# An encoder layer whose instruction order a planner sets: looser bounds on who takes a place, another first wave, and four more places

## The chip, the cores and the metric

The kernel runs on one core of a Trainium2 chip. The core has TensorE (PE in the profile, with its weight loads as PEld), VectorE (DVE), ScalarE (ACT), GpSimd (POOL), and SyncE (SP), which here issues nearly all DMAs. The metric is the device time of one execution in microseconds; the kernel before takes 2035.23 us (median of three runs, 2032.91 to 2036.42).

## The reference

One layer of an encoder on a sequence of 2048 tokens with 1024 features, in float32. The mixer is windowed attention with 16 query heads and 4 key/value heads, a sink logit for each head and a relative-position bias; a SwiGLU with 2816 hidden units follows. Shift, scale and gate of each sub-layer come from a conditioning vector `c` (adaLN):

```python
c_act = jax.nn.silu(c)
mod = (c_act @ ada_w[i] + ada_b[i])[:, None, :]
sh1, sc1, g1, sh2, sc2, g2 = jnp.split(mod, 6, axis=-1)
h = rmsnorm(x, mix_norm_pre[i]) * (1.0 + sc1) + sh1
y = windowed_gqa_sink(h, att_w_qkv[j], att_w_o[j], att_sink[j], rel_bias)
x = x + g1 * rmsnorm(y, mix_norm_post[i])
h = rmsnorm(x, ffn_norm_pre[i]) * (1.0 + sc2) + sh2
x = x + g2 * rmsnorm(swiglu(h, ffn_w_in[i], ffn_w_out[i]), ffn_norm_post[i])
```

`rmsnorm` divides by the root of the mean square over the 1024 features. `mod` is a product of a 1024-vector with a 1024x6144 matrix.

## The kernel before

**Layout.** Features lie on the 128 partitions, so a 512-token chunk of x is eight tiles of 128x512 (`x0_0` to `x0_7` for chunk 0), and there are four chunks. A product in float32 accuracy is made of three fast ones: each operand is split into a high part `hi` (a rounding cast on ACT) and a low part `lo` (the rest, a subtraction on DVE or POOL), and `three` issues w_hi·h_hi, w_hi·h_lo and w_lo·h_hi, each 128x512. A product of two plain float32 operands is also possible; the trace shows it as two records of a matmul.

**Stages.** (1) *The first wave.* Chunk 0 is loaded, squared on ACT, added in pairs on DVE, and three plain float32 matmuls with a matrix of ones sum the squares over the partitions (`squares0`, `rstd_of`). ACT and DVE make the reciprocal root `nr` of it. Then, for each of the eight feature tiles k: two rows of `ada_w` are loaded and reduced against silu(c) on DVE (`ada_reduce`, a custom instruction 1024 wide, which the trace calls CUSTOM_DVE_ANT_0) to give scale (`mod` 8+k, then `coef` k) and shift (`mod` k); 896 columns of the query/key/value weights for k are loaded and split (`w_piece`, tiles `w0_k`; the raw columns and the `ada_w` rows share five places, `raws`); x_k is multiplied by `nr` on DVE, scaled and shifted on ACT, and split; and 21 matmuls (seven output tiles by three) add feature tile k into seven PSUM banks. The remaining 640 columns (`w1_k`) come after. (2) The rest of the projections of chunks 0 and 1. (3) Attention in 64 units of 128 queries and one key/value head. Under its first half PE is filled up with the projections of chunks 2 and 3, under its second half with the output projections of chunks 0 to 2 (class `OProj`, tiles `ol` and `wo`): each unit pulls about 18 or 20 such matmuls (`Budget`, `FILL`). (4) `OProj` of a chunk writes eight tiles y, sums their squares (`yacc`, squares in `nsq` tiles), takes their norm (`nhio`, `nloo` are the two matmuls of that sum), adds x (`residual`), squares and sums again (`xacc`), takes the second norm (`nhix`, `nlox`), and makes the FFN's input h2 (`make_h2`), which goes through HBM. (5) The output projection of chunk 3, without attention beside it. (6) The FFN, with a Strassen-like scheme of seven products in place of eight, from about 700 us to the end.

**What sets the order.** None of the code above issues an instruction. `Recorder` notes every call in program order; `schedule` then runs a list scheduler (`forward`, with a cost in ns for each operation) and a backward pass that gives each operation a due time, eighteen times over, replays each order with random DMA delays, and keeps the best. `emit` writes the instructions in that order (line 748, so nearly every row of the profile has that line), with each on its engine's queue; an engine works its queue strictly in that order. Tiles with the same tag of the same pool share a number of places (`bufs`). In `forward` an operation that is the first to touch a tile can only be placed when the tile can have a place, and the places of a tag are given out strictly in recorded order:

```python
def slot_of(b):
    t = b.tag
    if t.order[t.next] is not b:
        return None
```

The PSUM pool `psF` has one tag, `mm`, with two banks. Under attention's second half its tiles are, in recorded order, the `py` tiles of the output projection (24 matmuls each) and, between them, the `nst` tiles of the norm sums. A `py` tile recorded behind a norm sum cannot take a bank before that norm sum has taken its own, which it does with its first matmul. In the pool `yp` the tag `y` has twelve places and `nsq`, the square tiles, four.

Of the kernel before, what the change touches and what calls it, by code (L numbers as in the profile page):

```python
# [20 lines left out]
P = 128  # L21
S = 2048
D = 1024
# [33 lines left out]

HOLD = 6
# [8 lines left out]
SPARE = 800.0  # L67

# [16 lines left out]
class Buf:  # L85


    def __init__(self, rec, name, shape, dtype, pool, tag):
# [3 lines left out]
        self.log, self.ops, self.slot, self.real = [], set(), None, None  # L92

# [42 lines left out]
class Recorder:  # L136
# [41 lines left out]
    def record(self, eng, fn, args, kw):  # L178
# [13 lines left out]
        if fn == "matmul" and not kw.get("start"):  # L192
            op.reads.append(op.writes[0])
        elif fn == "matmul":
            op.writes = [(op.writes[0][0], (3, (1 << P) - 1))]
# [13 lines left out]
        for w, items in ((False, op.reads), (True, op.writes)):  # L209
            for b, m in items:  # L210
# [3 lines left out]
                if b.tag is not None and op not in b.ops:  # L214
# [3 lines left out]
                    op.tiles.append(b)  # L218
        op.succ = []
# [26 lines left out]
    def cost(self, op, outs, ins):  # L246
# [12 lines left out]
        elif eng == "pe":  # L259
            if fn == "transpose":  # L260
                op.occ, op.lat = 108, 330
            elif outs[0].dtype == F32 and ins[0].dtype == F32:
                op.occ, op.lat = 860 * n // CH, 1060 * n // CH
# [79 lines left out]
    def forward(self, ahead, spare):  # L343


        for t in self.tags:
            t.next, t.held, t.free = 0, [None] * t.bufs, [0.0] * t.bufs
            t.parked = []
# [12 lines left out]
        def slot_of(b):  # L361
            t = b.tag
            if t.order[t.next] is not b:
# [53 lines left out]
        while n < len(ops):  # L417
# [119 lines left out]
            for b in o.tiles:  # L537
                t = b.tag
                b.end = max(b.end, end)
                if b.slot is None:  # L540
# [4 lines left out]
                    t.next += 1  # L545
                    wake(t)
# [209 lines left out]

def row(ap, n):
# [5 lines left out]
def encoder_layer(ctx, tc, a):  # L763
# [36 lines left out]
    gains = constr.tile([P, 4, KT], F32, name="gains")  # L800
    nsink = const.tile([P, HEADS], F32, name="nsink")
# [8 lines left out]
    def rstd_of(alloc, psp, ptag, acc, tag, r=None, direct=False, short=False, keep=False):  # L810
# [5 lines left out]
        if direct or len(sums) > 1:  # L816
            for i, sq in enumerate(sums):
                pe.matmul(ps, f(ones), sq, start=i == 0, stop=i == len(sums) - 1)
        else:
# [10 lines left out]
        if short:  # L830
# [3 lines left out]
            dve.scalar_tensor_tensor(out, t, 1.5, r, ALU.add, ALU.mult)  # L834
            return out
# [26 lines left out]
    class Chunk:  # L862
# [20 lines left out]
        def squares0(self):  # L883
# [6 lines left out]
            dve.tensor_tensor(sq[6], sq[4], sq[6], ALU.add)  # L890
            self.acc = [sq[0], sq[2], sq[6]]

        def norm(self, psp, ptag):
            r = nrm.tile([P, CH], F32, tag="nr", name=f"nr{self.c}")
            self.r = rstd_of(rot(nrm, "nsq", 2), psp, ptag, self.acc, f"a{self.c}", r)
# [41 lines left out]
    with ExitStack() as pa:  # L937
        w2 = open_pool(pa, "w2", side="right")
        raws = open_pool(pa, "raws", 5, side="right")
        w1 = open_pool(pa, "w1", side="right")  # L940
        psA = open_pool(pa, "psA", 8, space=PSUM)

        cb = nrm.tile([P, D], F32, name="cb")
        sp.dma_start(cb, row(a["c"], D))
        ch0 = Chunk(0)
        sp.dma_start(adab, a["ada_b"])
        sp.dma_start(gains, a["gains"])
        act.activation(cb, cb, AF.Silu)
# [9 lines left out]

        wres = {}
# [896 lines left out]
```

## Time and profile before

| | |
|---|---|
| median of three runs | 2035.23 us |
| the profiled execution, its own time | 2033.44 us |
| its span, first to last instruction | 2031.6 us |
| mean granted TensorE clock | 0.997 |
| PE, DVE, ACT, POOL busy in the span | 98%, 83%, 53%, 28% |
| DMA moved | 415.23 MB, mean 204 GB/s |

The page gives the busy share of each engine in 40 slices of some 51 us, the DMA queues, the chain of work that ended last and the costliest groups of instructions. A matmul's end is modelled, so PE counts as busy while matmuls follow one another at whatever spacing; the number of matmuls that start in a stretch, and the distance of their starts, tell more than the share.

### The profile page before, as it was taken

How to read it: one execution, taken by the hardware profiler on the slowest of the kernel's cores; microseconds unless marked ns; L12 is line 12 of the kernel's file. 1: busy time of each engine (PE TensorE's matmuls, PEld its weight loads, DVE VectorE, ACT ScalarE, POOL GpSimd, SP SyncE). 2: the span in 40 equal slices, each digit the busy share in tenths (PEclk: the TensorE clock that was granted, in tenths of full speed). 3: DMA queues.
4: the chain of work that ended last, by engine and by line, in shares of the span. 5: the costliest groups of instructions: out<-in, count | busy, mean ns of one | idle time of the engine just before them, and what ended most of it. 6: DMA issues, size and time to landing. Idle time of an engine off the chain costs nothing.

```text
span 2031.6 us, 29024 instructions
## 1 busy us (share of the span) xinstructions
PE 1995.9 (98%) x9392; PEld 1663.1 (82%) x9392; DVE 1689.8 (83%) x3051; ACT 1072.0 (53%) x2099; POOL 571.7 (28%) x520
## 2 busy tenths in 40 slices
PE   6999999999999999999999999999999999999999
PEld 4888888888787878788888888888888888888888
DVE  7868888877989888988887998776776789989997
ACT  5557766777778864344343533333333744455433
POOL 1302442344657513432333231111111000120034
PEclk9999999999999999999999999999999999999999
DMA  9895765576777694444446743333233794398543
GB/s 312 307 331 198 241 210 173 195 279 227 254 272 257 225 363 152 160 161 165 166 158 244 272 151 134 117 137 106 83 124 101 236 335 152 108 331 300 174 156 110
DMA packets 208581, 415.23 MB, mean 204 GB/s; under 512 B 19964, under 2 KB 61997, under 8 KB 205357
## 3 DMA queue, kind: packets, MB, share of 16 engines
q1 hardware_dynamic: 207852, 412.84, 59.1%
q8 instruction: 75, 1.23, 0.2%
q14 instruction: 78, 0.63, 0.1%
q10 hardware_dynamic: 576, 0.52, 0.1%
HBM read 278.52 MB, written 134.77 MB: 203 GB/s over the span
## 4 chain that ended last, share of the span: by engine, by line
PE 65%; DVE 2%; DMA 1%; issue 1%; ACT 0%; POOL 0%; SPq 0%; ACTq 0%; DVEq 0%; POOLq 0%
PE bank L748 65%; DMA hb<-h_d 0%; DVE pr L748 0%; DMA wor<-w_o 0%; DVE u_i L748 0%; DVE y L748 0%; DVE plo L748 0%; DMA ly<-y_d 0%; DMA lx<-xT 0%; DVE ly L748 0%; POOL ly L748 0%; DVE ws_i L748 0%; DVE wa_i L748 0%; SPq L748 0%; DVE of L748 0%
## 5 line engine op out<-in xcount | busy, mean ns | idle before, releaser
L748 PE MATMUL bank<-ht,ws_i 128*128 128x512 f32 x1584 | 374.0, 389 | 0.0
L748 PEld LDWEIGHTS bank<-ht,ws_i 128*128 128x128 f32 x1584 | 297.3, 188 | 61.7
L748 PE MATMUL bank<-hb,wa_i 128*128 128x512 f32 x1056 | 254.1, 389 | 0.5 <-DVE hb L748 0.5
L748 PEld LDWEIGHTS bank<-hb,wa_i 128*128 128x128 f32 x1056 | 198.1, 188 | 42.0 <-DVE hb L748 0.9
L748 PE MATMUL bank<-ol,wo 128*128 128x512 f32 x768 | 206.1, 396 | 2.1 <-ACT yacc L748 1.1
L748 DVE TENSOR_TENSOR u_i<-bank,u_i 128x512 f32<-128x512 f32 x176 | 120.9, 688 | 80.3 <-PE bank L748 77.7
L748 ACT CAST ws_i<-s_i 128x512 fp32r<-128x512 f32 x132 | 81.9, 621 | 192.9 <-DVE s_i L748 96.8
L748 ACT ACTIVATE pr<-pr,nm 128x385 f32<-128x385 f32 (+1 forms) x256 | 154.8, 606 | 53.2 <-DVE nm L748 48.0
L748 DVE CUSTOM_DVE_ANT_0 pr<-bank,bias,nsink 128x384 f32<-128x384 f32 (+1 forms) x256 | 149.8, 594 | 25.3 <-PE bank L748 21.7
L748 POOL TENSOR_SCALAR pr<-pr,rs 128x384 f32<-128x384 f32 (+1 forms) x177 | 114.6, 660 | 179.7 <-DVE rs L748 167.9
L748 PEld LDWEIGHTS bank<-ol,wo 128*128 128x128 f32 x768 | 141.2, 188 | 28.5 <-ACT yacc L748 1.5
L748 POOL TENSOR_TENSOR p_i<-p_i,u_i 128x512 f32<-128x512 f32 x41 | 66.9, 1633 | 346.3 <-DVE u_i L748 176.0
L748 POOL TENSOR_TENSOR z<-z,z 128x512 f32<-128x512 f32 x28 | 43.8, 1572 | 337.4 <-ACT ws_o L748 263.2
L748 PE MATMUL bank<-k,q 128*128 128x384 f32 (+1 forms) x512 | 135.4, 344 | 1.5 <-DVE nm L748 1.4
L748 PE MATMUL bank<-hi,ws 128*128 128x512 f32 x384 | 134.3, 400 | 0.0
L748 DVE TENSOR_TENSOR plo<-bank,phi 128x512 fp32r<-128x512 f32 x184 | 120.7, 684 | 11.2 <-ACT phi L748 10.1
L748 ACT CAST wa_i<-wiri 128x512 fp32r<-128x512 f32 x132 | 81.3, 620 | 90.8 <-PE bank L748 77.6
L748 PE MATMUL bank<-hb,ws_i 128*128 128x512 f32 x528 | 126.9, 389 | 1.6 <-ACT p_i L748 1.6
L748 PE MATMUL bank<-ht,wa_i 128*128 128x512 f32 x528 | 126.8, 389 | 0.0
L748 DVE TENSOR_TENSOR z<-bank,z 128x512 f32<-128x512 f32 (+1 forms) x164 | 107.7, 659 | 17.9 <-PE bank L748 16.5
L748 DVE TENSOR_TENSOR wa_i<-wiri,wa_i 128x512 fp32r<-128x512 f32 x132 | 103.8, 788 | 19.1 <-ACT wa_i L748 19.1
L748 PEld LDWEIGHTS bank<-hb,ws_i 128*128 128x128 f32 x528 | 99.0, 188 | 22.5 <-ACT p_i L748 2.0
(275 smaller groups left out, 4434.5 us busy)
## 6 DMA issues: line engine op xcount, KB each, us to landing
wiri<-w_in SPq DMA_DIRECT2D x88, 512.0 KB, 4.6
ada<-ada_w SPq DMA_DIRECT2D x40, 512.0 KB, 5.3
q_d<-e SPq DMA_DIRECT2D x32, 512.0 KB, 4.6
q<-q_d SPq DMA_DIRECT2D x16, 1024.0 KB, 7.0
wo<-wo_d SPq DMA_DIRECT2D x16, 1024.0 KB, 6.0
wiro<-w_out SPq DMA_DIRECT2D x40, 384.0 KB, 4.4
g_d_b<-p_i SPq DMA_DIRECT2D x44, 256.0 KB, 3.4
g_d_t<-p_i SPq DMA_DIRECT2D x40, 256.0 KB, 2.0
```

The lines of the kernel that those rows point to most:

```text
L748: o.ins = getattr(engs[o.eng], o.fn)(*args, **kw)
```

## The change

Three things at once.

1. *Places in the order of readiness, within bounds.* For the tags listed in `LOOSE` (`psF`'s `mm` and `yp`'s `nsq`, each 4) a tile may take a place ahead of up to four that were recorded before it, but not ahead of one of its own family (names that begin with the same letters: `py`, `nst`, `psq`). All other tags stay strict.
2. *A new first wave.* The rows of `ada_w` get a pool of their own with sixteen places (`raws0`), and the pool of the `w1_k` tiles is opened when it closes, in the same space. For k = 0 (`ADA_PE = 1`) shift and scale are plain float32 matmuls with one moving column: eight for each, on a copy of `ada_w` laid out for it, and silu(c) as a 128x8 tile `ct`. The low parts of the `w0_k` split are fixed on DVE. The squares are summed in four matmuls in place of two additions and three matmuls. The norm's chain is the short form (one ACT square less). For chunk 0 `hi` is written by ACT straight from the scaled x, with a second activation for x itself, in place of an activation and a cast. And `busy` adds matmuls that nobody reads, into a PSUM tile `warm`: 14 at the start, 6 behind the first sum of squares, 5 and 8 behind two DVE steps of the norm.
3. *Sixteen places* for `y` in place of twelve.

```diff
+ADA_PE = 1
+WARM = {"ones": 14, 0: 6, "t": 5, "r": 8}
+LOOSE = {("psF", "mm"): 4, ("yp", "nsq"): 4}
...
+            t.left = list(t.order)
+            skip = LOOSE.get((t.pool.name, t.name), 0)
+            t.reach = skip + 1
...
             t = b.tag
-            if t.order[t.next] is not b:
+            for x in t.left[:t.reach]:
+                if x is b:
+                    break
+                if x.family == b.family:
+                    return None
+            else:
                 return None
...
+            if fill is not None:
+                fill("t", t)
+                fill("r", r)
             return out
...
-            dve.tensor_tensor(sq[6], sq[4], sq[6], ALU.add)
-            self.acc = [sq[0], sq[2], sq[6]]
+            self.acc = sq[::2]
...
-            act.activation(xt, xt, AF.Identity, bias=mod[:, k:k + 1], scale=coef[:, 0, k:k + 1])
+            if c == 0:
+                act.activation(hi, xt, AF.Identity, bias=mod[:, k:k + 1], scale=coef[:, 0, k:k + 1])
+            act.activation(xt, xt, AF.Identity, bias=mod[:, k:k + 1], scale=coef[:, 0, k:k + 1])
+            if c == 0:
+                return scaled, dve.tensor_tensor(lo, xt, f(hi), ALU.subtract)
...
-        w2 = open_pool(pa, "w2", side="right")
         raws = open_pool(pa, "raws", 5, side="right")
         w1 = open_pool(pa, "w1", side="right")
+        first = ExitStack()
+        raws0 = open_pool(first, "raws0", KT * C2 * 2 // D, side="right")
...
+        def ada_products(k):
+            for e, t in enumerate((8 + k, k)):
+                w = raws0.tile([P, D], F32, tag="raw", name=f"adat{t}")
+                sp.dma_start(w, a["ada_t"][t])
+                j = 2 * k + e
+                for i in range(KT):
+                    pe.matmul(ada_ps[:, j:j + 1], w[:, i * P:(i + 1) * P], ct[:, i:i + 1],
+                              start=i == 0, stop=i == KT - 1)
+                dve.tensor_tensor(mod[:, t:t + 1], ada_ps[:, j:j + 1], adab[:, t:t + 1], ALU.add)
...
-            split(t[:, 0], t[:, 1], w[:, :n], pool)
+            split(t[:, 0], t[:, 1], w[:, :n], pool if i else dve)
...
+        def busy(what, src):
+            for _ in range(WARM.get(what, 0)):
+                pe.matmul(warm[:, :P], f(ones), src[:, :P], start=True, stop=True)
...
-                y = yp.tile([P, CH], F32, tag="y", name=f"y{c}_{n}", bufs=4 if c == NCH - 1 else 12)
+                y = yp.tile([P, CH], F32, tag="y", name=f"y{c}_{n}", bufs=4 if c == NCH - 1 else 16)
```

The planner draws the whole order anew from this, so nearly every queue differs. Three places follow, each as the queue stood and as it stands now.

*PE, the start of the program, before* (`nsq` are the pairs of squares, `hi0_0` is feature tile 0 of chunk 0):

```order
L748 MATMUL bank0<-nsq0_0_86,ones_57 128x512
L748 MATMUL bank0<-nsq0_2_95,ones_57 128x512
L748 MATMUL bank0<-nsq0_6_115,ones_57 128x512
L748 MATMUL bank1<-hi0_0_164,w0_0_137 128x512
L748 MATMUL bank2<-hi0_0_164,w0_0_137 128x512
```

*and in the change* (`adat` are the rows of `ada_w` for k = 0; the matmuls into bank0 up to `hi0_0` are the ones nobody reads):

```order
L767 MATMUL bank0<-ones_57 128x128 x14
L767 MATMUL bank1<-nsq0_0_103,ones_57 128x512
L767 MATMUL bank0<-nsq0_0_103,ones_57 128x128 x6
L767 MATMUL bank1<-nsq0_2_114,ones_57 128x512
L767 MATMUL bank1<-nsq0_4_128,ones_57 128x512
L767 MATMUL bank1<-nsq0_6_138,ones_57 128x512
L767 MATMUL bank2<-mod_64,adat8_105 128x1 x8
L767 MATMUL bank2<-mod_64,adat0_112 128x1 x8
L767 MATMUL bank0<-nta0_175,ones_57 128x128 x5
L767 MATMUL bank0<-nr0_154,ones_57 128x128 x8
L767 MATMUL bank3<-hi0_0_206,w0_0_173 128x512
```

Behind the sums of squares there are now 16 one-column matmuls and 13 unread ones before the first projection.

*DVE in the first wave, before* (`ISA ada` is the reduction of a row of `ada_w`, `ISA mod` reads its sum, `lo` and `w0` are low parts of a split):

```order
L748 TENSOR_TENSOR lo0_0_176<-x0_0_64,hi0_0_164 128x512
L748 TENSOR_TENSOR x0_2_72<-x0_2_72,nr0_129 128x512
L748 TENSOR_TENSOR w0_2_180<-wqkv2_0_150,w0_2_180 128x896
L748 ISA ada11_162,mod_132<-ada11_162,cb_84,adab_88 128x1024
L748 ISA mod_132 128x1
L748 ISA ada2_146,mod_132<-ada2_146,cb_84,adab_88 128x1024
L748 ISA mod_132 128x1
L748 ISA ada10_139,mod_132<-ada10_139,cb_84,adab_88 128x1024
L748 ISA mod_132 128x1
L748 TENSOR_TENSOR lo0_1_220<-x0_1_70,hi0_1_194 128x512
L748 SCALAR_TENSOR_TENSOR coef_152<-mod_132,gains_117 128x1
L748 TENSOR_TENSOR x0_3_74<-x0_3_74,nr0_129 128x512
```

*and in the change:*

```order
L767 TENSOR_TENSOR lo0_0_225<-x0_0_71,hi0_0_206 128x512
L767 SCALAR_TENSOR_TENSOR coef_186<-mod_64,gains_131 128x1
L767 TENSOR_TENSOR x0_1_75<-x0_1_75,nr0_154 128x512
L767 TENSOR_TENSOR w0_1_220<-wqkv1_0_145,w0_1_220 128x896
L767 ISA ada10_149,mod_64<-ada10_149,cb_126,adab_101 128x1024
L767 ISA mod_64 128x1
L767 TENSOR_TENSOR lo0_1_253<-x0_1_75,hi0_1_236 128x512
L767 ISA ada2_158,mod_64<-ada2_158,cb_126,adab_101 128x1024
L767 ISA mod_64 128x1
L767 SCALAR_TENSOR_TENSOR coef_186<-mod_64,gains_131 128x1
L767 TENSOR_TENSOR x0_2_78<-x0_2_78,nr0_154 128x512
L767 TENSOR_TENSOR w0_2_255<-wqkv2_0_167,w0_2_255 128x896
```

Before, some low parts of the weights are missing here (k = 1, 5, 6 and 7 stood in POOL's queue); now DVE's queue goes round with the same six operations, and the two reads of a sum, for k = 1 to 4: reduction, `lo`, reduction, `coef`, x, `w0`.

*PE under attention's second half, around the second norm sum of chunk 0 (`nhix0`, `nlox0`), before* (`ol,wo` is output projection, all other rows but the norm sum are attention):

```order
L748 MATMUL bank7<-plo9_3_2_5721,v2_3_5120 128x512
L748 MATMUL bank4<-ident_59,pr10_3_5513 128x128
L748 MATMUL bank5<-ident_59,pr10_3_5513 128x128
L748 MATMUL bank6<-ident_59,pr10_3_5513 128x128
L748 MATMUL bank3<-k3_0_5308,q3_0_5301 128x384 x2
L748 MATMUL bank2<-k3_0_5308,q3_0_5301 128x384 x2
L748 MATMUL bank1<-nhix0_5747,ones_57 128x512
L748 MATMUL bank0<-ol1_0_4217,wo1_4_5528 128x512 x4
L748 MATMUL bank1<-nlox0_5750,ones_57 128x512
L748 MATMUL bank0<-ol1_0_4217,wo1_4_5528 128x512 x2
```

*and in the change:*

```order
L767 MATMUL bank1<-ol1_2_5099,wo1_5_5645 128x512 x4
L767 MATMUL bank3<-k3_0_5360,q3_0_5356 128x384 x2
L767 MATMUL bank1<-ol1_2_5099,wo1_5_5645 128x512
L767 MATMUL bank5<-ident_59,pr10_3_5541 128x128
L767 MATMUL bank4<-ident_59,pr10_3_5541 128x128
L767 MATMUL bank6<-ident_59,pr10_3_5541 128x128
L767 MATMUL bank1<-ol1_3_5126,wo1_5_5645 128x512 x3
L767 MATMUL bank0<-nhix0_5847,ones_57 128x512
L767 MATMUL bank5<-ident_59,pr10_3_5541 128x128
L767 MATMUL bank1<-ol1_3_5126,wo1_5_5645 128x512 x2
```

Before, no `ol,wo` row stands in the 27 rows ahead of `nhix0`: the next one, `wo1_4`, begins right behind it. Now `wo1_4` and `wo1_5` begin ahead of the norm sum; behind `nlox0` one more `ol,wo` row stands, and then 17 rows of attention alone up to `wo1_6`.

More of the change, by code (lines that the diff above doesn't have):

```diff
@@ L218, in record @@
                     op.tiles.append(b)
+        if eng == "pe" and op.writes[0][0].group is not None:
+            for q in op.writes[0][0].group:
+                op.pred.setdefault(q, 0)
+            op.writes[0][0].group = [op]
         op.succ = []
@@ L970, in w_piece @@
                 wres[k, "v"] = (t[:, 0, :2 * P], t[:, 1, :2 * P])
+        warm = psA.tile([P, CH], F32, tag="mm", name="warm")
+        def busy(what, src):
+            for _ in range(WARM.get(what, 0)):
+                pe.matmul(warm[:, :P], f(ones), src[:, :P], start=True, stop=True)
+        busy("ones", f(ones))
         ch0.squares0()
-        ch0.norm(psA, "mm")
+        ch0.norm(psA, "mm", busy)
         steps = []
```

38 lines of the change are left out of this document (30 added, 8 removed).

## The prediction

> **What bounds the kernel now.** I read the page first, then the chain, then windows by stage, then the timeline where the windows show a loss.
>
> ```profile
> span 2031.6 us, 29024 instructions
> PE 1995.9 (98%) x9392; PEld 1663.1 (82%) x9392; DVE 1689.8 (83%) x3051; ACT 1072.0 (53%) x2099; POOL 571.7 (28%) x520
> 841.41 1177.96 PE bank L748 x5280
> ```
>
> PE is the bound: busy 98%, and from 841 us to 2019 us the chain is one unbroken run of matmuls. The change hardly touches those, so a gain can only come from the 36 us in which PE idles and from matmuls that run at half clock. The windows say where both are:
>
> ```profile
> 0.00:50.00 50.00, 29.70 (x99) 19.80 (x100) 38.33 (x63) 28.02 (x37) 6.83 (x9) 1.00 0.91 312
> 50.00:54.00 4.00, 4.00 (x12) 3.13 (x11) 4.00 (x4) 0.95 (x2) 1.34 (x1) 0.57 0.82 269
> 550.00:560.00 10.00, 7.18 (x29) 4.83 (x28) 8.68 (x22) 7.30 (x17) 7.34 (x7) 0.77 0.79 265
> 560.00:570.00 10.00, 9.80 (x44) 7.79 (x43) 8.28 (x20) 4.86 (x12) 6.50 (x8) 0.89 0.59 206
> 600.00:620.00 20.00, 20.00 (x111) 17.24 (x110) 18.56 (x48) 16.00 (x39) 7.16 (x11) 1.00 0.80 275
> 640.00:660.00 20.00, 18.20 (x96) 14.43 (x96) 19.73 (x52) 18.34 (x45) 15.80 (x17) 1.00 0.87 282
> 690.00:720.00 30.00, 27.47 (x117) 21.27 (x116) 24.77 (x30) 22.56 (x35) 12.83 (x9) 1.00 1.00 364
> 1000.00:1200.00 200.00, 200.00 (x884) 165.62 (x883) 175.29 (x247) 84.58 (x142) 65.47 (x43) 1.00 0.59 208
> ```
>
> The columns are stretch, length, then busy time and count of PE, PEld, DVE, ACT and POOL, granted clock, DMA share, GB/s. Four places lose time: the start (20 us), 550 to 570 (73 matmuls where a full 20 us holds some 110, and a clock of 0.77 and 0.89), 640 to 660, and 690 to 720.
>
> **Part 1, the first wave.** How the norm reaches the first projection, and what holds PE afterwards:
>
> ```profile
> 13.29 2.04 PE L748 MATMUL bank<-nsq,ones 128*128 128x512 f32 x2 [1.33 <-DVE nsq L748]
> 15.37 0.69 ACT L748 ACTIVATE nr<-bank,epsc 128x512 f32<-128x512 f32 x1
> 15.99 0.94 ACT L748 CAST w<-wqkv 128x896 fp32r<-128x896 f32 x1
> 16.84 0.63 ACT L748 ACTIVATE nr<-nr 128x512 f32<-128x512 f32 x1
> 17.49 0.63 ACT L748 ACTIVATE nta<-nr 128x512 f32<-128x512 f32 x1
> 18.16 0.69 DVE L748 SCALAR_TENSOR_TENSOR nta<-bank,nta 128x512 f32<-128x512 f32 x1
> 18.76 1.27 DVE L748 CUSTOM_DVE_ANT_0 ada<-ada,cb,adab 128x1024 f32<-128x1024 f32 x1
> 22.73 0.62 ACT L748 CAST hi<-x 128x512 fp32r<-128x512 f32 x1
> 23.40 3.25 PE L748 MATMUL bank<-hi,w 128*128 128x512 f32 x7 [8.07 <-ACT hi L748]
> 30.15 1.27 DVE L748 CUSTOM_DVE_ANT_0 ada<-ada,cb,adab 128x1024 f32<-128x1024 f32 x1
> 31.36 0.68 DVE L748 TENSOR_TENSOR lo<-x,hi 128x512 fp32r<-128x512 f32 x1
> 31.96 0.14 DVE L748 SCALAR_TENSOR_TENSOR coef<-mod,gains 128x1 f32<-128x1 f32 x1
> 32.03 0.68 DVE L748 TENSOR_TENSOR x<-x,nr 128x512 f32<-128x512 f32 x1
> 32.63 0.14 DVE L748 SCALAR_TENSOR_TENSOR coef<-mod,gains 128x1 f32<-128x1 f32 x1
> 32.83 1.09 DVE L748 TENSOR_TENSOR w<-wqkv,w 128x896 fp32r<-128x896 f32 x1
> 33.84 1.28 DVE L748 CUSTOM_DVE_ANT_0 ada<-ada,cb,adab 128x1024 f32<-128x1024 f32 x1
> 45.55 3.21 DVE L748 CUSTOM_DVE_ANT_0 ada<-ada,cb,adab 128x1024 f32<-128x1024 f32 x1
> 45.58 2.10 POOL L748 TENSOR_TENSOR w<-wqkv,w 128x896 fp32r<-128x896 f32 x1 [20.59 <-DMA ada<-ada_w]
> 49.43 0.50 PE L748 MATMUL bank<-lo,w 128*128 128x512 f32 x1 [2.44 <-DVE lo L748]
> ```
>
> *The start.* Out of the chain from 15.37 to 23.40 go a weight cast (15.99 to 16.84, 0.85 us), the ACT square (0.67), a reduction on DVE (1.20, from 18.76 to its successor) and the `hi` cast (0.67): 3.4 us. Into it come the low part of `w0_0` ahead of x on DVE (1.0) and some 0.2 for the wider second step: 2.2 us net. Ahead of it the second pair addition goes (0.7), and a last sum of squares at full clock takes half of 2.04 (1.0); the loads stand one small DMA later (0.4): 1.3. Against it, DVE's queue now has the `mod` addition of the one-column products ahead of the norm's steps. No row shows such a product; the nearest are the two records of a float32 sum above, 2.04 us with 512 columns, and a one-column matmul still loads its weights twice:
>
> ```profile
> 9.88 0.50 PEld L748 LDWEIGHTS bank<-nsq,ones 128*128 128x128 f32 x2 [3.59 <-DVE nsq L748]
> ```
>
> Eight such products are then at most 8 x 0.50 = 4 us and, with loads at full clock, 2; the addition is late by 0.6 to 2.6, and I take 1.5, nearer to the full clock because the unread matmuls run PE on from 1 us. Those stand ahead of the sums in PE's queue: at a quarter of 2.04 us each, 14 last until 8.2, and six with the first sum until 13.3; three sums more end at 19.4 if the clock stays at half, 4 us later than before; at full clock from 8 us on they end ahead of the last pair of squares, and cost nothing. [...] First projection: 23.4 - 2.2 - 1.3 + 1.5 = 21.4.
>
> *The pace.* From the starts of the DVE rows one k takes two reductions (1.21 each), `lo` 0.60, `coef` 0.07, x 0.60 and `w0` 1.01: 4.7 us. PE needs 21 matmuls at 0.226 (884 in the 200 us from 1000), 4.75. Before, POOL's subtractions stood beside it, and a DVE row with one beside it took 3.21 instead of 1.28. In the change POOL does nothing until the `w1` pieces. So PE can run through k = 0 to 6 (147 matmuls, 33.2 us) from 21.4 with about 1 us of waiting: 55.6. For k = 7, adding up DVE's queue from x0_0 at 19.7 gives its `lo` at 57; two `w1` subtractions on POOL meet it then, 2 us each by the row at 45.55, so 57 to 61. I take 59; 13 value matmuls and seven `hi` fill PE until then. DMA isn't in the way: what is needed until `w0_7` is 14.7 MB (x 2.1, 16 rows of `ada_w` 8.4, eight weight pieces 3.7, c 0.5), which at the 312 GB/s of the first 50 us lands by 49. The wave is done at about 62.
>
> ```profile
> L748 PE MATMUL bank<-hi,w x91: 388/389/796, 23.4 to 60.6; 128*128 128x512 f32 x91
> L748 PE MATMUL bank<-lo,w x43: 387/389/628, 26.5 to 62.0; 128*128 128x512 f32 x43
> ```
>
> Before, 134 of the wave's 168 had begun by 62. The 34 others are 7.7 us. **Take -7**; bounds -9.5 (no collision) and -1 (the norm 4 us late by unread matmuls at half clock, and a third collision, 2).
>
> [...] The row at 49.43 shows PE waiting 2.44 us, and the window behind it a clock of 0.57. [...] By the trace it costs 0.43 x 4 = 1.7 us more, which the bound holds.
>
> **Part 2, the looser places.**
>
> ```profile
> 550.83 0.47 PE L748 MATMUL bank<-ol,wo 128*128 128x512 f32 x1
> 555.11 0.61 PE L748 MATMUL bank<-ident,pr 128*128 128x128 f32 x3 [1.25 <-DVE pr L748]
> 556.82 1.12 PE L748 MATMUL bank<-ident,pr 128*128 128x128 f32 x4 [1.11 <-POOL pr L748]
> 563.42 0.50 PE L748 MATMUL bank<-nhix,ones 128*128 128x512 f32 x1 [0.20 <-DVE nhix L748]
> ```
>
> From 550.83 until the norm sum at 563.42 PE has no output projection, since the next `py` tile stands behind that sum; attention alone waits for DVE and POOL, 2.6 us in these rows, and the clock falls: (0.23 + 0.11) x 10 = 3.4 us more. The order now puts `wo1_4` and `wo1_5` there, and all but 17 rows of attention have such cover. The 6 us can go whole, or stay if the 17 rows wait as the 27 did. **Take -4.5**, since 17 bare rows last too short for most of it. At 640 to 660, 15 matmuls are missing against 600 to 620, at 0.18 us 2.7; the same pattern stands ahead of the second chunk's sum. Bounds -3 to +2; **take -1.5**. The sixteen places cost no instruction; they let `py` run on while residuals hold their y, and are in these figures.
>
> **Part 3, behind attention.** There the second chunk's norm sum has moved: 74 matmuls, not 215, lie between `nlox1` and the FFN's first matmul. **Take 0**, bounds -2.5 (the idle of 690 to 720) and +8 (the rival below). Elsewhere the new order may make or remove small waits, 2 us either way.
>
> Sum: -7 - 4.5 - 1.5 = -13 on the profiled 2033.44 is 2020.4. The median of the runs lies 1.8 higher, by which it is 2022.2. I count from the middle of the two, 2034.3: the forecast is **2021.5 us** (rounded up by 0.2).
>
> **The rivals.** *(a) Slower, by the FFN's start.*
>
> ```profile
> 665.11 0.48 PE L748 MATMUL bank<-nlox,ones 128*128 128x512 f32 x1
> 712.27 1.04 SPq L748 DMA_DIRECT2D hd_d_t<-y  x2
> 699.53 7.67 DMA hb<-h_d
> ```
>
> From `nlox1` to the last of these stores took 48 us, and a load behind them up to 7.7: 56. PE has 15 us (74/215 of the 43 before), then 192 output projections (43.6) and three FFN matmuls for cover: 60. If the stretch, at a DMA share of 1.00, grows by more than 4 us, PE waits; from 17 us on the gain is gone. At 25 us it is 2042. Against it: attention no longer slows DVE there. Chance 0.07. *(b) The start pays alone*: the 17 rows wait as the 27 did, or the gain returns as a smaller wait at the FFN: 2034.3 - 6.5 = 2028; 0.15. *(c) The change doesn't do what it says at the start*, because four POOL collisions, or unread matmuls at half clock, leave `lo7` as late as PE's backlog was: the middle alone, 2034.3 - 6 = 2028; 0.10. *(d) All at the good bound*: -9.5 - 6 - 3: 2015; 0.10. The forecast, 2016 to 2027, has 0.58.
>
> **How the numbers follow.** About 0.2%, 4 us, is what a measurement of this kernel can tell from no change. Faster: 0.58 + 0.10, and 0.18 of the 0.25 of (b) and (c): 0.86. Within: their other 0.07. Slower: 0.07. The range that leaves out 0.1 at each end is 2012 to 2031: below it only (d) with the FFN's idle gone too, above it (a) and the weak ends of (b) and (c).
>
> **What would show it.** Right: `hi,w` begins at 20 to 22.5; CUSTOM_DVE rows of 1.28 up to 45 us; no half clock at 50 or 550; over 100 matmuls in the 20 us around `nhix0`. Wrong: a wait of PE for `nsq` or `mod` past 22.5, a second 3 us wait in the first wave, waits for `ht` or `hb` tiles of several us between 680 and 760, or new waits between 70 and 540 us, where there is next to none.

## The result

| | before | after |
|---|---|---|
| median of four runs | 2035.2 us (2032.91 to 2036.42) | 2023.4 us (2023.06 to 2024.51) |
| profiled execution, its own time | 2033.44 | 2024.51 |
| its span | 2031.6 | 2022.7 |

The ratio is 0.9943, with a 95% interval of 0.9928 to 0.9958: faster by 11.8 us. The two profiled executions are only 8.9 us apart, since that of before lies 1.8 below its median and that of after 1.1 above. All that is read from traces below has to add up to some 9, not to 12.

One correction to the part on the change: the pool `raws0` has ten places (8·640·2/1024, the room of `w2`), not sixteen. Sixteen are the places of `y` alone.

The first lines of the page of the changed kernel, and its windows (columns as in the prediction):

```profile
span 2022.7 us, 29224 instructions
PE 2003.4 (99%) x9492; PEld 1673.9 (83%) x9492; DVE 1693.7 (84%) x3042; ACT 1079.3 (53%) x2100; POOL 565.0 (28%) x526
```

```profile
0.00:50.00 50.00, 46.92 (x230) 39.01 (x231) 37.05 (x67) 30.16 (x39) 0.70 (x6) 0.97 0.90 347
50.00:54.00 4.00, 4.00 (x19) 3.33 (x18) 3.96 (x6) 3.45 (x7) 2.14 (x2) 1.00 0.83 242
550.00:560.00 10.00, 10.00 (x54) 8.63 (x54) 8.39 (x22) 8.21 (x20) 7.67 (x8) 1.00 0.55 170
560.00:570.00 10.00, 10.00 (x61) 8.59 (x59) 8.44 (x21) 7.01 (x18) 4.42 (x7) 1.00 1.03 369
640.00:660.00 20.00, 18.40 (x103) 14.58 (x102) 19.12 (x49) 15.49 (x39) 16.10 (x19) 1.00 0.76 239
690.00:720.00 30.00, 25.08 (x102) 18.30 (x101) 26.29 (x26) 22.41 (x34) 14.37 (x8) 1.00 1.02 353
160.00:180.00 20.00, 17.28 (x77) 12.62 (x76) 18.85 (x43) 17.29 (x36) 1.66 (x3) 1.00 0.88 323
```

Between 550 and 570 us 115 matmuls begin where 73 did, at full clock. But 690 to 720 has 102 where it had 117, and 160 to 180 has 77 where the same view of before shows this:

```profile
160.00:180.00 20.00, 20.00 (x100) 16.97 (x99) 16.94 (x39) 15.06 (x34) 5.16 (x7) 1.00 0.67 206
```

**A ledger of lost time.** Windows of two kernels at one time show different work, since after a first gain everything is earlier. So I compare at equal work: each matmul of the layer counts with the distance of starts in its unbroken runs (0.227 us for 512 columns, 0.175 for 384, 0.120 for 256, 0.109 for 128); the first wave's sums of squares, its one-column products and the unread matmuls count nothing. The time at which a matmul begins, less the work ahead of it, is the time lost until there. In us, lost within stretches of work; the whole is 1965.9 us of work:

| us of work | what lies there | before | after | change |
|---|---|---|---|---|
| 0 to 60 | first wave | 30.7 | 23.8 | -6.9 |
| 60 to 140 | projections | 0.7 | 0.6 | -0.1 |
| 140 to 250 | start of attention | 3.6 | 7.5 | +3.9 |
| 250 to 500 | attention | 2.5 | 3.0 | +0.5 |
| 500 to 640 | the two norm sums | 13.0 | 5.9 | -7.1 |
| 640 to 720 | ahead of the FFN | 3.6 | 7.3 | +3.7 |
| 720 to 1960 | FFN | 1.8 | -0.3 | -2.1 |

The first wave and the norm sums gained 14.0 us; the start of attention and the stretch ahead of the FFN gave back 7.6. The changes add up to -8.1; the other 0.8 of the 8.9 lies behind 1960 us of work.

### The profile page after: what moved, and what is told of

The parts are those of the page before. It is cut to its first block, busy times and chain, and to the rows that moved or that the text cites. A ratio compares the mean times of both kernels' runs of the same rounds, so it can differ in the third digit from the quotient of the medians.

```text
span 2022.7 us, 29224 instructions
## 1 busy us (share of the span) xinstructions
PE 2003.4 (99%) x9492; PEld 1673.9 (83%) x9492; DVE 1693.7 (84%) x3042; ACT 1079.3 (53%) x2100; POOL 565.0 (28%) x526
## 4 chain that ended last, share of the span: by engine, by line
PE 92%; DVE 4%; DMA 2%; issue 1%; ACT 1%; SPq 0%; POOL 0%; ACTq 0%; DVEq 0%; POOLq 0%
PE bank L767 92%; DVE ada L767 1%; DVE pr L767 1%; DMA h_d<-y 1%; DVE z L767 0%; DMA bias<-tab_d 0%; DMA hb<-h_d 0%; SPq L767 0%; DMA x<-xT 0%; DVE plo L767 0%; ACT y L767 0%; ACT pr L767 0%; DVE x L767 0%; DMA out<-zx 0%; DMA zx<-x_d 0%
## 5 line engine op out<-in xcount | busy, mean ns | idle before, releaser
L767 PE MATMUL bank<-ol,wo 128*128 128x512 f32 x768 | 210.8, 398 | 4.2 <-DVE wo L767 1.8
L767 POOL TENSOR_TENSOR p_i<-p_i,u_i 128x512 f32<-128x512 f32 x39 | 61.2, 1568 | 353.0 <-DVE u_i L767 147.0
L767 DVE TENSOR_TENSOR plo<-bank,phi 128x512 fp32r<-128x512 f32 x184 | 121.0, 685 | 13.1 <-ACT phi L767 11.5
L767 ACT CAST phi<-bank 128x512 fp32r<-128x512 f32 x184 | 102.5, 588 | 27.3 <-PE bank L767 25.1
L767 PEld LDWEIGHTS bank<-ht,wa_i 128*128 128x128 f32 x528 | 99.1, 188 | 20.6
```

What stands on the lines that cost most here:

```text
L767: o.ins = getattr(engs[o.eng], o.fn)(*args, **kw)
```

## The experiments

Twelve kernels; their places are told together in a table at the end of this part. Each one is drawn anew by the planner (its order of all instructions is called a draw below), and this turned out to matter as much as the edits. The kernel before, run again beside them, had medians from 2033.9 to 2035.2 us, so a total is compared with another session's to about 1 us.

**The first wave.** What of its many edits pays? First one edit alone:

```diff
 # the kernel before
-            split(t[:, 0], t[:, 1], w[:, :n], pool)
+            split(t[:, 0], t[:, 1], w[:, :n], pool if i else dve)
```

> The kernel before with the low parts of the w0 pieces fixed on DVE, and nothing else. Theory T1 (POOL's subtractions beside DVE's rows made the waits at 45 to 53 us): the 2.44 us wait and the half clock behind it go, the first projection stays at 23 to 24, the loss up to 60 us of work falls from 30.7 to 26 to 28, and the time is 2031, between 2029 and 2033. Rival (the low parts lengthen DVE's queue by what the collisions cost): within 1.5 us of 2034.6.

Measured: 2034.61 us, ratio 1.0003 (0.9994 to 1.0013), and the first wave loses 24.5, against 30.7 before and 23.8 with all the edits. In the groups of its stretch from 20 to 62 us the reductions are undisturbed; in the same view of before they took 1546 ns each:

```profile
L748 DVE CUSTOM_DVE_ANT_0 ada<-ada,cb,adab 128x1024 f32<-128x1024 f32 x14 | 17.5, 1280 | 0.0
```

```profile
L748 DVE CUSTOM_DVE_ANT_0 ada<-ada,cb,adab 128x1024 f32<-128x1024 f32 x14 | 21.5, 1546 | 0.0
```

In its place the theory holds, with a larger size than written: one edit is 6.2 us of gain, of which 0.65 is an earlier start (the first projection is at 22.75). The total shows none of it, and is where the rival had it. The start of attention, 250 to 500, the norm sums and the stretch ahead of the FFN together lose 28.7 us where before loses 22.7. Nothing of the edit lies there; the order was drawn anew. The counterpart takes that edit out of the changed kernel:

```diff
 # the changed kernel
-            split(t[:, 0], t[:, 1], w[:, :n], pool if i else dve)
+            split(t[:, 0], t[:, 1], w[:, :n], pool)
```

> The changed kernel with the low parts of the w0 pieces free to go to POOL again, as before. Theory T1 (POOL's subtractions slow DVE's rows beside them from 1.28 to 3.21 us, and so the first wave): waits of PE for lo tiles of 2 to 3 us between 40 and 62 us are back, and the time is 2 to 4 us longer, 2025.5 to 2027.5. [...]

Measured: 2040.05 us, ratio 1.0024 to before (1.0014 to 1.0033): 16.7 us slower than the changed kernel, and all of it in the first wave (40.3 lost in place of 23.8). The same groups, and PE's waits of over 2 us in that stretch (start, length, in brackets the idle ahead); from 40 to 48 us the clock was 0.57:

```profile
L767 DVE CUSTOM_DVE_ANT_0 ada<-ada,cb,adab 128x1024 f32<-128x1024 f32 x12 | 24.3, 2044 | 0.0
L767 POOL TENSOR_TENSOR w<-wqkv,w 128x896 fp32r<-128x896 f32 x8 | 22.2, 2788 | 27.4 <-DVE nr L767 19.8 <-ACT w L767 5.1 <-DVE x L767 2.6
```

```profile
31.99 1.91 PE L767 MATMUL bank<-hi,w 128*128 128x512 f32 x7 [2.39 <-ACT hi L767]
43.47 0.79 PE L767 MATMUL bank<-lo,w 128*128 128x512 f32 x1 [4.78 <-DVE lo L767]
52.66 0.50 PE L767 MATMUL bank<-lo,w 128*128 128x512 f32 x1 [2.26 <-DVE lo L767]
58.52 1.90 PE L767 MATMUL bank<-hi,w 128*128 128x512 f32 x7 [2.24 <-ACT hi L767]
```

POOL took eight subtractions (1.01 us each on DVE's queue), and the 12 reductions of that stretch took 2.04 in place of 1.28. Both engines lost. The theory holds; my 2 to 4 us were at least four times too small. This draw gave POOL all eight pieces, where before gave it four.

```diff
 # the changed kernel
-WARM = {"ones": 14, 0: 6, "t": 5, "r": 8}
+WARM = {}
```

> The changed kernel without the matmuls that nobody reads. Theory T1 (they keep the clock at full when the sums and the first projections come): the first seven projections take 3.2 us in place of 1.86, the norm sums are later by 1 us, and the time is 2 to 3.5 us longer, 2025 to 2027. Rival (DVE's pace bounds the first wave and PE catches up by k = 3): less than 1 us longer.

Measured: 2025.55 us (ratio 0.9956, 0.9939 to 0.9972), 2.1 above the changed kernel; the first wave loses 25.7, 1.9 more. Without the unread matmuls the first seven projections take 3.36 us, as the timeline shows; in the changed kernel they are the second row, 1.86 us:

```profile
22.32 3.36 PE L767 MATMUL bank<-hi,w 128*128 128x512 f32 x7 [2.71 <-ACT hi L767]
```

```profile
21.93 1.86 PE L767 MATMUL bank<-hi,w 128*128 128x512 f32 x7
```

The theory holds: the 33 unread matmuls together are worth 2 us.

```diff
 # the changed kernel
-ADA_PE = 1
+ADA_PE = 0
```

> The changed kernel with shift and scale of k = 0 reduced on DVE as for the other k (no one-column products on TensorE). Theory T1 (the products take 2.4 us of reductions off DVE's queue, and DVE sets the first wave's pace): the first wave is 1 to 2.5 us longer and the time 2024.5 to 2026. Rival (DVE waits for the norm's steps at that time anyway, and the reductions fit in there): first projection not later than 22, and the time within 1 us of 2023.4.

Measured: 2027.43 us (0.9963, 0.9949 to 0.9977), 4.0 above; the first wave loses 29.1, 5.3 more. The first projection comes at 23.06, 1.1 later, so the rival falls; but the theory's 1 to 2.5 us are too few as well. What it left out are two short waits of PE at 56 to 58 us, and the low clock that sets in behind the first (0.57 in 56 to 64 us):

```profile
56.29 0.45 PE L767 MATMUL bank<-w,hi 128*128 128x256 f32 x1 [1.24 <-DMA wqkv<-w_qkv]
58.23 0.58 PE L767 MATMUL bank<-w,hi 128*128 128x256 f32 x1 [1.07 <-POOL w L767]
```

```profile
56.00:64.00 8.00, 6.64 (x19) 5.25 (x20) 8.00 (x5) 5.59 (x8) 8.00 (x5) 0.57 0.70 227
```

**The looser places.** Out of the changed kernel, and alone in the kernel before:

```diff
 # the changed kernel
-LOOSE = {("psF", "mm"): 4, ("yp", "nsq"): 4}
+LOOSE = {}
```

> The changed kernel with all tags strict again (the first wave and the sixteen places stay). Theory T2 (the 7 us gained around the first norm sum, at about 550 us, come from the looser places): the half-clock stretch at 550 to 560 us is back, and the time is 2023.4 + 7 = 2030, between 2028 and 2033. Rival (the new order as a whole, drawn from a different first wave, would have covered that stretch anyway): 2022 to 2026.

Measured: 2028.51 us (0.9969, 0.9959 to 0.998), 5.1 above the changed kernel. 500 to 640 us of work lose 13.4 again in place of 5.9, and ahead of the FFN 4.7 in place of 7.3. The time is as expected, and so is the size; the hole is there again, 86 matmuls between 550 and 570, though made of waits and not of a low clock.

```profile
550.00:570.00 20.00, 17.63 (x86) 13.22 (x86) 19.33 (x49) 16.05 (x38) 14.00 (x18) 1.00 0.68 239
```

```diff
 # the kernel before, with the edits of the first and third place of LOOSE's code
+LOOSE = {("psF", "mm"): 4, ("yp", "nsq"): 4}
...
-                y = yp.tile([P, CH], F32, tag="y", name=f"y{c}_{n}", bufs=4 if c == NCH - 1 else 12)
+                y = yp.tile([P, CH], F32, tag="y", name=f"y{c}_{n}", bufs=4 if c == NCH - 1 else 16)
```

> The kernel before with the looser places and the sixteen places for y, and nothing else; its first wave and its pools stay. T2: the loss at 515 to 520 us of matmul work goes (-7), nothing new comes at the start of attention (T3), and the time is 2035.2 - 7 = 2028, between 2025 and 2030. Rival (the first wave carries the whole gain): 2033 to 2037.

Measured: 2032.51 us, ratio 0.9992 (0.9983 to 1.0002): no difference, so less gain than was expected. But 500 to 640 us of work lose 4.7 in place of 13.0, 8.3 less, with 104 matmuls in the window in place of 73:

```profile
550.00:570.00 20.00, 20.00 (x104) 16.47 (x103) 17.66 (x41) 15.11 (x36) 14.50 (x15) 1.00 0.91 296
```

It is given back twice: 3.8 in the first wave, whose instructions are those of before in another order (ACT's queue, for one, now has silu(c), 1.06 us with a table load of 1.28 ahead of it, in front of the last three squares), and 7.9 ahead of the FFN. The second isn't only chance, as the table shows. The sixteen places are a condition of the looser ones: with twelve y, or with `psF` alone loosened, the planner comes to a point at which no operation can be placed. By themselves they close nothing: strict has them, and loses 13.4.

**The start of attention.** In the trace of after, the chain of waits from 160 us on, SP's issues, and the rows that waited:

```profile
162.13 8.88 DMA bias<-tab_d
```

```profile
153.87 0.37 SPq L767 DMA_DIRECT2D q<-q_d  x1
162.13 0.37 SPq L767 DMA_DIRECT2D bias<-tab_d  x1
```

```profile
171.15 0.48 DVE L767 CUSTOM_DVE_ANT_0 pr<-bank,bias,nsink 128x256 f32<-128x256 f32 x1 [0.75 <-DMA bias<-tab_d]
171.70 0.91 PE L767 MATMUL bank<-k,q 128*128 128x256 f32 x4 [0.93 <-DVE nm L767]
174.33 0.62 PE L767 MATMUL bank<-k,q 128*128 128x384 f32 x2 [0.52 <-DVE nm L767]
```

Before, the first q was loaded at 103 us and the bias tables from 127 on. The cause suggests itself: the change puts the pools in the order `raws`, `w1`, `raws0` (later `w2`), where it was `w2`, `raws`, `w1`. Attention's pools start at the same end, so the first bias table and q, k and v now lie over `w1`, whose tiles chunk 1's last projections read. This was theory T3, with one experiment in each direction:

```diff
 # the changed kernel; the ada_w rows become tiles of w2, tag "w2"
+        w2 = open_pool(pa, "w2", KT, side="right")
         raws = open_pool(pa, "raws", 5, side="right")
         w1 = open_pool(pa, "w1", side="right")
-        first = ExitStack()
-        raws0 = open_pool(first, "raws0", KT * C2 * 2 // D, side="right")
...
-        first.close()
-        w2 = open_pool(pa, "w2", side="right")
```

> The changed kernel with the ada_w rows and the w1_k tiles in one pool of eight places of 5 KB that lies at the near end of the memory's stack, so that raws and w1 take the places they had in the kernel before. Theory T3 (the 5 us that the changed kernel loses at the start of attention, 155 to 178 us, come from where its pools lie: the first bias table and the first q, k and v tiles lie over weights that are read last): their loads are issued early again, that loss is gone, and the time is 2023.4 - 5 = 2018, between 2017 and 2020. Rival (the loss is chance, one of the small waits that any new order makes): a loss of 2 to 6 us stays between 155 and 180 us or shows up at another place, and the time is 2022 to 2026. Eight places in place of ten for the ada_w rows should cost the first wave less than 1 us by either.

Measured: 2021.41 us (0.9936, 0.9922 to 0.9951). The loads are early again (q at 94 us, bias from 119), and the start of attention loses 2.6 in place of 7.5. Three small changes elsewhere (+1.3 at 60 to 140, -1.6 at the norm sums, +1.3 ahead of the FFN) are the draw's. By this run alone T3 would be shown.

```diff
 # the kernel before
-        w2 = open_pool(pa, "w2", side="right")
         raws = open_pool(pa, "raws", 5, side="right")
         w1 = open_pool(pa, "w1", side="right")
+        w2 = open_pool(pa, "w2", side="right")
```

> The kernel before with one line moved: the pool of the w1_k tiles (w2) is opened after raws and w1, not ahead of them, so that the pools lie as in the changed kernel; nothing else. T3: the loads of the first bias table and of q, k and v of the first unit are issued only after 155 us, PE waits for the bias table at about 170 us, 4 to 5 us are lost between 140 and 160 us of matmul work, where the kernel before loses 0.2, and the time is 2039, between 2037 and 2041. Rival (the order of the pools does not matter by itself): less than 1.5 us lost there, 2033 to 2036.

Measured: 2034.94 us, ratio 1.0002 (0.9993 to 1.0011). The loads are late, as in the changed kernel, and nothing is lost: 2.5 at the start of attention, and PE without a gap.

```profile
162.58 1.24 SPq L748 DMA_DIRECT2D q<-q_d  x2
170.32 0.42 SPq L748 DMA_DIRECT2D bias<-tab_d  x1
```

```profile
160.00:180.00 20.00, 20.00 (x91) 16.33 (x90) 17.14 (x31) 12.28 (x21) 0.00 (x0) 1.00 0.96 338
```

So T3 as I had it falls. The order of the pools makes the loads late, in every one of the seven kernels that has it. Whether PE waits for them is decided by what the planner puts behind the first scores: here PE does 25 projections of chunks 2 and 3 after its first four score matmuls; in after it does 11, and then ten score matmuls in a row, which wait for DVE again and again (the rows above), the first time because DVE waits for the bias table. (In after the first four, too, wait 0.55 us, for a load of k.)

**Ahead of the FFN.** In the traces of before, of after and of most of the experiments PE's last waits there are for one tile: attention's last output goes to HBM (`o_d<-of`) and comes back as `ol3_3`, which chunk 3's output projection needs. In after attention's last matmul begins at 685.8, and:

```profile
687.85 1.06 SPq L767 DMA_DIRECT2D o_d<-of  x1
696.66 0.32 SPq L767 DMA_DIRECT2D ol<-o_d  x1
```

```profile
704.87 3.46 PE L767 MATMUL bank<-ol,wo 128*128 128x512 f32 x14 [0.95 <-DVE ol L767]
```

The way takes 19 us (before: 692.3 to 711.7, as long). For cover PE has what is left of chunk 2's projections, 17 matmuls in after and 31 before, and of chunk 3 only the 18 of each tile that don't need `ol3_3`, of two tiles, since two have banks: 53 x 0.227 = 12 us in after, 67 x 0.227 = 15.2 before. 19.1 - 12 = 7.1 and 19.4 - 15.2 = 4.2, against 7.3 and 3.6 lost. The loss is counted over the same stretch, so that this sum comes out near it says little; the test is to give the wait more cover. This is theory T4, and one more tile should give 4.1 us:

```diff
 # one_pool
+    psC = open_pool(ctx, "psC", 6, space=PSUM)
     lasto = ExitStack()
...
-                ps = psF.tile([P, CH], F32, tag="mm", name=f"py{c}_{n}")
+                ps = psC.tile([P, CH], F32, tag="p", name=f"py{c}_{n}") if c == NCH - 1 and n == 2 else psF.tile(
+                    [P, CH], F32, tag="mm", name=f"py{c}_{n}")
...
-                w = wop.tile([P, 2, KT, P], F32R, tag="w", name=f"wo{c}_{n}", bufs=2)
+                w = wop.tile([P, 2, KT, P], F32R, tag="w", name=f"wo{c}_{n}", bufs=3 if c == NCH - 1 else 2)
```

> The kernel with one pool (one_pool, 2021.4), and three tiles of chunk 3's output projection under way at once in place of two: the third has a bank of the FFN's six, and the weights wo have three places. Theory T4 (the 7 to 12 us lost ahead of the FFN in the kernels with looser places are the way of attention's last output through HBM, some 19 us, less the output projections that PE still has by then; the third tile brings 18 more, 4.0 us): the loss between 640 and 670 us of work falls from 8.6 to 4 to 5, and the time is 2017, between 2015 and 2018.5. Rival (the stretch is bound by its transfers, DMA share 1.0 from 690 us on): the third tile's weights are late as well, and the time is 2020 to 2023.

Measured: 2019.21 us (0.9921, 0.9906 to 0.9936). Between 640 and 670 us of work 5.3 are lost in place of 8.6, between the theory's number and the rival's; 1.1 more until 720 and 2.3 in the FFN take back what the norm sums gained (1.8), and more. The wait is the same one, 2.23 us in place of 3.19:

```profile
694.31 22.04 PE L767 MATMUL bank<-ol,wo 128*128 128x512 f32 x89 [2.23 <-ACT ol L767]
```

```diff
 # third_bank
-... if c == NCH - 1 and n == 2 else psF.tile(
+... if c == NCH - 1 and n in (2, 3) else psF.tile(
...
-bufs=3 if c == NCH - 1 else 2)
+bufs=4 if c == NCH - 1 else 2)
```

> The kernel with one pool and a third tile (third_bank, 2019.2), with a fourth tile of chunk 3's output projection under way as well, and four places for its weights. Theory T4: 18 more matmuls, 4.0 us, cover the way of attention's last output; the loss between 640 and 670 us of work falls from 5.4 to 2 to 3, and the time is 2016.5, between 2015 and 2018. Rival (what is left there isn't that way but the transfers, or the weights of the fourth tile come late): 2018.5 to 2021.

Measured: 2018.71 us (0.9922, 0.9907 to 0.9937), a miss, in the range of the rival: not to be told from third_bank, though below the changed kernel by 4.7. 3.6 are lost between 640 and 670, in place of the 2 to 3 expected. The cover grew, and so did the way: attention's last matmul is at 682.4, its store is issued only at 689.46, and the wait is over at 705.45, after 23 us in place of 19.

```profile
689.46 0.52 SPq L767 DMA_DIRECT2D o_d<-of  x1
697.09 0.48 SPq L767 DMA_DIRECT2D ol<-o_d  x1
```

```profile
705.45 10.85 PE L767 MATMUL bank<-ol,wo 128*128 128x512 f32 x45 [1.45 <-ACT ol L767]
```

T4 stands as the cause of the wait: each added tile shortened the loss. Its size was foreseen only in part (3.3 of 4.1 us, then 1.7 of 4.0), since the way is drawn anew too.

**The draw.** The same instructions, with one number of the planner changed:

```diff
 # the changed kernel
-SPARE = 800.0
+SPARE = 1000.0
```

> The changed kernel with one number of the planner changed, its allowance for late loads (1000 ns in place of 800), so that it draws another order of the same instructions. Theory (first wave and looser places are worth what the change's own runs show, and the losses at the start of attention and ahead of the FFN are a matter of the draw): the loss up to 60 us of work stays within 1.5 of 23.8, none comes between 500 and 550, the start of attention loses 1 to 5, the stretch ahead of the FFN 4 to 9, and the time is 2019 to 2027. Rival (the gains too are a matter of the draw): the loss up to 60 us of work is above 26, or 4 us and more are lost between 500 and 550.

Measured: 2027.41 us (0.9964, 0.9951 to 0.9977), 4.0 above the changed kernel and just above the upper edge of what was written. The first wave loses 23.7, as it should. 500 to 550 us of work lose 3.4 and the 20 behind them 2.6 more, in place of next to nothing: for the norm sums, 7.2 until 640, still 6 below the strict orders. The start of attention loses 2.9 with pools that lie as in after, which speaks against T3 once more; ahead of the FFN it is 12.0, beyond the 4 to 9 expected, with nothing of chunk 2 left as cover when attention ends:

```profile
691.52 0.50 PE L767 MATMUL bank<-ol,wo 128*128 128x512 f32 x1 [3.45 <-DVE ol L767]
```

Last, the edits that had paid in their places, without the others:

```diff
 # the kernel before
+ low parts of w0 on DVE; LOOSE with sixteen y; third tile of chunk 3 (all as above)
```

> The kernel before with three edits: the low parts of the w0 pieces fixed on DVE, the looser places with sixteen y, and the third tile of chunk 3's output projection. Products, unread matmuls, four sums, short norm and direct cast of the new first wave stay out, and the pools lie as before. Theory: in the first wave the one edit on DVE is nearly all of the gain (loss up to 60 us of work 24 to 25.5, against 23.3 with the whole new wave), 500 to 640 us of work lose 2 to 7 in place of 13, the stretch ahead of the FFN 4 to 6, and the time is 2020.5, between 2018 and 2023.5. Rival (the rest of the new first wave is worth more than 3 us, which w0_dve_alone hid by a lucky draw): above 2023.5, with the difference to third_bank in the first 60 us of work.

Measured: 2027.6 us (0.997, 0.9957 to 0.9982), a miss in the total. The first wave loses 25.4 and the norm sums 3.5, as written. Ahead of the FFN 3.5 until 670 us of work, but 5.8 between there and 720, where the FFN's first tiles are late (`hb`, `ht`), and the ten matmuls from 751.84 us on take 4.14 us, where nine at 744.86 us took 2.20:

```profile
747.64 0.50 PE L759 MATMUL bank<-hb,ws_i 128*128 128x512 f32 x1 [0.58 <-DVE hb L759]
750.35 1.01 PE L759 MATMUL bank<-ht,ws_i 128*128 128x512 f32 x2 [1.28 <-ACT ht L759]
751.84 4.14 PE L759 MATMUL bank<-ht,ws_i 128*128 128x512 f32 x10 [0.48 <-DVE ht L759]
```

The rival had the time and not its place: of the 8.4 us to third_bank 2.1 lie in the first 60 us of work, and 2.9 between 640 and 720.

All of them, in us lost by stretches of work, and the medians:

| kernel | 0-60 | 60-140 | 140-250 | 250-500 | 500-640 | 640-720 | 720-1960 | median |
|---|---|---|---|---|---|---|---|---|
| *strict places* | | | | | | | | |
| before | 30.7 | 0.7 | 3.6 | 2.5 | 13.0 | 3.6 | 1.8 | 2035.2 |
| w0_dve_alone | 24.5 | 0.8 | 3.6 | 3.9 | 13.7 | 7.5 | 0.8 | 2034.6 |
| late_pools | 30.9 | 0.6 | 2.5 | 3.9 | 13.2 | 5.4 | 1.0 | 2034.9 |
| strict | 24.1 | 0.6 | 5.6 | 3.7 | 13.4 | 4.7 | -0.3 | 2028.5 |
| *looser places* | | | | | | | | |
| after | 23.8 | 0.6 | 7.5 | 3.0 | 5.9 | 7.3 | -0.3 | 2023.4 |
| redraw | 23.7 | 0.6 | 2.9 | 3.9 | 7.2 | 12.0 | 1.0 | 2027.4 |
| cold | 25.7 | 0.6 | 7.4 | 3.0 | 5.6 | 7.5 | -0.3 | 2025.6 |
| no_products | 29.1 | 0.6 | 4.2 | 4.0 | 4.1 | 6.4 | 0.5 | 2027.4 |
| w0_pool | 40.3 | 0.6 | 4.2 | 3.1 | 6.6 | 8.2 | 0.9 | 2040.1 |
| loose_alone | 34.5 | 0.8 | 2.6 | 2.9 | 4.7 | 11.5 | 2.0 | 2032.5 |
| one_pool | 23.1 | 1.9 | 2.6 | 3.0 | 4.3 | 8.6 | -0.2 | 2021.4 |
| *and more tiles of chunk 3* | | | | | | | | |
| few_edits | 25.4 | 0.9 | 3.3 | 4.1 | 3.5 | 9.3 | 1.3 | 2027.6 |
| third_bank | 23.3 | 1.9 | 2.6 | 3.0 | 2.5 | 6.4 | 2.1 | 2019.2 |
| fourth_bank | 23.6 | 1.9 | 2.6 | 3.0 | 5.6 | 5.1 | -0.1 | 2018.7 |

Read by columns. Strict places lose 13.0 to 13.7 at the norm sums, looser ones 2.5 to 7.2, in ten kernels without an exception: this gain is the edit's. Ahead of the FFN, with two tiles, strict orders lose 5.3 on the mean (3.6 to 7.5) and looser ones 8.8 (6.4 to 12.0), so 3.5 of some 8 come back there. The first have 27 to 38 of chunk 2's matmuls left when attention ends, the others none to 24: by these counts, what filled the hole at 550 us was the cover of the wait at 700. The count isn't all, since w0_dve_alone has 28 left and loses 7.5. In the first wave the edits don't add up singly: without the products 5.3 more are lost, without the unread matmuls 1.9, and few_edits, which has neither, loses only 1.6 more than after. The start of attention loses 2.6 to 3.6 with early loads and 2.5 to 7.5 with late ones.

## Why the prediction was right and wrong

**The time** was 1.9 us above the forecast and within the case that had 0.58. More than half of that closeness is luck: on the profiled executions the forecast was -13, and -8.9 came, 4.1 off. The medians lie further apart, by 11.8, only because of where those executions stand among the runs.

**Part 1 (-7; measured -6.9).** Right in size and in its main mechanism: without POOL's subtractions the reductions take 1.28 us and DVE keeps PE's pace. The first projection came at 21.93 for a forecast of 21.4, but not by the way that the working had. The products were late by the least that was thought possible: the sixteen products are 32 records with a weight load each, and 18 of them take 2.06 us, 0.11 each, or 1.8 us for eight; the addition that waits for them delays the norm's next step to 15.68, where ACT's step ahead of it was done at 15.05 (14.42 and 0.63): 0.6 late, not 1.5:

```profile
13.50 2.06 PE L767 MATMUL bank<-mod,adat 128*128 128x1 f32 x18
...
14.42 0.63 ACT L767 ACTIVATE nr<-nr 128x512 f32<-128x512 f32 x1
...
15.60 0.16 DVE L767 TENSOR_TENSOR mod<-bank,adab 128x1 f32<-128x1 f32 x1 [3.12 <-PE bank L767]
15.68 0.68 DVE L767 SCALAR_TENSOR_TENSOR nta<-bank,nr 128x512 f32<-128x512 f32 x1
```

With the products late by 0.6 alone, `hi` of the first feature tile is written by 20.33, a us ahead of the 21.4. What then holds PE is what the working put at nothing: the eight unread matmuls behind `nr`. They stand ahead of the first projection in PE's queue, and from 18.2 to 21.4 us the clock is 0.50:

```profile
19.05 3.13 PE L767 MATMUL bank<-nr,ones 128*128 128x128 f32 x16
19.52 0.81 ACT L767 ACTIVATE hi<-x,mod,coef 128x512 fp32r<-128x512 f32 x1 [1.27 <-DVE mod L767]
21.93 1.86 PE L767 MATMUL bank<-hi,w 128*128 128x512 f32 x7
```

The working had counted only the twenty ahead of the sums. In strict, redraw, third_bank and fourth_bank the first projection comes 3.1 to 3.2 us behind its `hi`, again right behind these eight, at 22.9 to 23.9, and the first wave loses 23.3 to 24.1 there all the same: PE makes up for the start within the wave. No run leaves out these eight alone.

At k = 7 PE waited 1.40 us, for a `w1` piece of POOL rather than for `lo7`:

```profile
60.36 0.38 PE L767 MATMUL bank<-w,hi 128*128 128x256 f32 x1 [1.40 <-POOL w L767]
```

What the working did not see is how uneven the parts are: one line alone brings 6.2 where all of them bring 6.9.

**Part 2 (-4.5 and -1.5; measured -7.1 and 0).** Both terms were mis-sized. The first left 1.5 of 6 us to the 17 bare rows, and nothing of the loss stayed: 0.2 us between 500 and 520 us of work, where before lost 7.3. The 6 was too small as well. By the starts of its matmuls before lost 7.1 between 551 and 564 us: 3.7 at its waits, of which the rows shown had 2.6, and the rest at the low clock. The second term was drawn from a likeness ("the same pattern stands ahead of the second chunk's sum"), and 530 to 640 us of work lose 5.6 before and after.

**Part 3 (0, bounds -2.5 and +8; measured +3.7).** The rival's direction, not its mechanism. I counted the stores and loads of h2 on their way to the FFN; the wait that decides is for attention's last output on its way to chunk 3's projection, and its cover is what the looser places use up earlier. The rows for that were in the trace of before: the way was there, 19 us, and 67 matmuls against it.

**Elsewhere (0, 2 either way; measured +2.2 in all).** The start of attention, +3.9, falls under what the prediction said would show it wrong, new waits between 70 and 540 us. The step that failed is that the pools' order was read as room for `raws0` alone: which pool comes to lie over which, and so which loads can be early, wasn't looked at. By late_pools and redraw this alone costs nothing; with an order that has no other matmuls behind the first scores it cost up to 4.6 (after against redraw). The FFN's -2.1 (before has a wait of 1.56 us at 841 us) I put down to the draw too: the others lie between -0.3 and 2.1 there.

**Still open:** why the planner's draws differ as they do. Its choices at 160 and 700 us can be told from each trace, not foreseen from an edit.

## What to carry to other kernels

Where a planner draws the whole order, judge an edit by the time lost at equal work, place by place: here one line was worth 6.2 us in its place and 0.6 in the total, and one number of the planner moved the total by 4. Filler that closes one hole is taken from another: look for the last wait of the program that the same work covers, and give that wait more (more tiles under way) before taking it away. And an operation moved off the engine that sets the pace is no gain if it slows that engine from beside: eight subtractions, 8 us of DVE's queue, cost 16 us on POOL.

## What the runs showed of the hardware

The clock fell to half behind waits of PE that were short: before, behind one of 2.44 us (0.50 from 50.5 to 53.5 us), and in no_products behind one of 1.24 us (0.57 in 56 to 64 us). There two matmuls of 256 columns begin 0.22 us apart at 56.53 us, where 0.12 is their distance in unbroken runs, already ahead of the second wait (1.07 us, up to 58.23), and those of 512 columns begin 0.43 apart until 63.31. But one of 1.40 us in after left it at full:

```profile
56.00:64.00 8.00, 6.60 (x34) 5.26 (x33) 6.33 (x7) 5.17 (x9) 7.82 (x5) 1.00 0.69 234
```

So did three longer ones in w0_pool, of 2.39, 2.26 and 2.24 us: the clock is 1.00 from 25 to 40 and from 48 to 64 us. The length of a single wait doesn't decide it, and what does isn't shown here.
